# Rotary embedding: a write of zeros replaced by an early store of two rows through SyncE

## The chip, the cores and the metric

The kernel runs on one core of a Trainium2 chip. The metric is the device time of one execution in microseconds (us). Before the change the median of three runs is 319.21 us (318.87 to 319.9).

The engines that matter here are VectorE (DVE), which does the arithmetic; ScalarE (ACT), which casts; GpSimd (POOL), which only issues transfers; and SyncE (SP), which also only issues transfers. Sixteen DMA engines move all the data, whichever engine issued the transfer. Only transfers issued by POOL change the number type on the way here: loads turn float32 into float16, stores turn float16 into float32.

## The reference

The input x has the shape (8, 2048, 16, 64): batch, position, head, element. Each head's 64 elements are two halves of 32, which are rotated by an angle of the position:

```python
x1 = x[..., :32]
x2 = x[..., 32:]
out1 = x1 * cos - x2 * sin
out2 = x1 * sin + x2 * cos
out = concatenate([out1, out2], axis=-1)
```

cos and sin have the shape (2048, 32) and serve all batches and heads. The input is 64 MB of float32, and so is the output. The arithmetic in the kernel is in float16.

## The kernel before

A tile is one batch. The 2048 positions are spread over 128 partitions, J = 16 consecutive positions ("rows") for each, so a partition holds 16 x 16 x 64 = 16384 elements of a batch: 64 KB in HBM as float32, 32 KB on chip as float16. Five buffers `xt` rotate through the eight batches (`NBUF = 5`).

- **Loads.** `load(b)` (line 53) is one transfer issued by POOL. The first five are issued at the start. For batch 0 it leaves out the first `JA = 2` rows of each partition. Those come as float32 through SyncE into a buffer `head` (line 36), and ScalarE casts them into the tile (line 78). SyncE then loads the sine and cosine tables (lines 45 and 46), which ScalarE casts to float16, the sine with both signs (lines 82 to 84).
- **Rotation.** `rotate` is four DVE instructions on a whole tile: second halves times minus sine (line 70) and first halves times sine (line 71) go into a scratch buffer `v`, the tile is multiplied in place by cosine (line 73), and `v` is added (line 75). There is one buffer `v`, so the tiles follow one another.
- **Stores.** `store(b)` (line 61) is one transfer issued by POOL for batches 0 to 6. Batch 7 goes out in three parts: rows 0 to 8 (line 109), rows 9 to 13 (line 111), both through POOL, and the last two rows, which ScalarE casts into `head` (line 119) and SyncE stores as float32 once the first part has landed (line 120).
- **The write of zeros.** POOL fills a small buffer `zero` (line 86). ScalarE issues a write of it, 128 elements (512 bytes) for each partition, to the start of that partition's rows of out[0] (line 87), once load 3 has landed: `add_manual_dep` adds that wait. Store 0 writes the same place later, so it waits until the zeros have landed.

The order on each engine isn't the program's order. When the TileContext closes, a planner goes through the instructions with costs of its own. When an engine's queue comes free in its reckoning, it places the earliest in program order of those that it reckons ready there. Semaphores for the data dependences are put in afterwards. So in the program load 5, which needs the buffer of batch 0 and so store 0's landing, comes right after store 0, while on POOL the order is: loads 0 to 4, stores 0 and 1, loads 5 and 6, stores 2 and 3, load 7, stores 4, 5 and 6, and the parts of batch 7. The transfers of POOL run through one queue (q0 in the profile), those of SyncE through q1, those of ScalarE through q10. An engine that waits at an instruction holds up everything behind it on the same engine.

Of the kernel before, what the change touches and what calls it, by code (L numbers as in the profile page):

```python
# [1 line left out]

# [4 lines left out]


@with_exitstack  # L10
def kernel(
    ctx: ExitStack,
    tc: tile.TileContext,
    x: bass.AP,
    cos: bass.AP,
    sin: bass.AP,
    out: bass.AP,
):
    nc = tc.nc
    f16 = mybir.dt.float16  # L20
    f32 = mybir.dt.float32

    B, S, H, D = x.shape
    Dh = D // 2
    P = nc.NUM_PARTITIONS
    J = S // P
    NBUF = 5

    const_pool = ctx.enter_context(tc.tile_pool(name="rope_const", bufs=1))
    io_pool = ctx.enter_context(tc.tile_pool(name="rope_io", bufs=NBUF))  # L30
    tmp_pool = ctx.enter_context(tc.tile_pool(name="rope_tmp", bufs=1))

    JA = 2
    head = const_pool.tile([P, JA, H, D], f32)
    x0 = x[0].rearrange("(p j) h d -> p j (h d)", j=J)
    nc.sync.dma_start(  # L36
        out=head.rearrange("p j h d -> p (j h d)"),
        in_=x0[:, 0:JA, :].rearrange("p j f -> p (j f)"),
    )
    sin_f = const_pool.tile([P, J, Dh], f32)  # L40
    cos_f = const_pool.tile([P, J, Dh], f32)
    cos_h = const_pool.tile([P, J, Dh], f16)
    sin_h = const_pool.tile([P, J, Dh], f16)
    neg_h = const_pool.tile([P, J, Dh], f16)
    nc.sync.dma_start(out=sin_f, in_=sin.rearrange("(p j) d -> p j d", j=J))  # L45
    nc.sync.dma_start(out=cos_f, in_=cos.rearrange("(p j) d -> p j d", j=J))

    loads = []

    def load(b):  # L50
        xt = io_pool.tile([P, J, H, D], f16)
        j0 = JA if b == 0 else 0
        dma = nc.gpsimd.dma_start(  # L53
            out=xt[:, j0:J, :, :].rearrange("p j h d -> p (j h d)"),
            in_=x[b].rearrange("(p j) h d -> p j (h d)", j=J)[:, j0:J, :].rearrange("p j f -> p (j f)"),
        )
        loads.append(dma)
        return xt

    def store(b, xt):  # L60
        nc.gpsimd.dma_start(  # L61
            out=out[b].rearrange("(p j) h d -> p (j h d)", j=J), in_=xt
        )

    def rotate(xt):
        v = tmp_pool.tile([P, J, H, D], f16)
        sin_b = sin_h.unsqueeze(2).to_broadcast([P, J, H, Dh])
        neg_b = neg_h.unsqueeze(2).to_broadcast([P, J, H, Dh])
        cos_b = cos_h.unsqueeze(2).to_broadcast([P, J, 2 * H, Dh])
        nc.vector.tensor_mul(out=v[:, :, :, 0:Dh], in0=xt[:, :, :, Dh:D], in1=neg_b)  # L70
        nc.vector.tensor_mul(out=v[:, :, :, Dh:D], in0=xt[:, :, :, 0:Dh], in1=sin_b)  # L71
        xw = xt.rearrange("p j h (e d) -> p j (h e) d", d=Dh)
        nc.vector.tensor_mul(out=xw, in0=xw, in1=cos_b)  # L73
        xa = xt.rearrange("p j h d -> p (j h d)")
        nc.vector.tensor_add(out=xa, in0=xa, in1=v.rearrange("p j h d -> p (j h d)"))  # L75

    tiles = [load(b) for b in range(NBUF)]
    nc.scalar.copy(  # L78
        out=tiles[0][:, 0:JA, :, :].rearrange("p j h d -> p (j h d)"),
        in_=head.rearrange("p j h d -> p (j h d)"),  # L80
    )
    nc.scalar.copy(out=sin_h, in_=sin_f)  # L82
    nc.scalar.mul(out=neg_h, in_=sin_f, mul=-1.0)  # L83
    nc.scalar.copy(out=cos_h, in_=cos_f)  # L84
    zero = const_pool.tile([P, 128], f32)
    nc.gpsimd.memset(zero, 0.0)  # L86
    blank = nc.scalar.dma_start(
        out=out[0].rearrange("(p j) h d -> p (j h d)", j=J)[:, 0:128], in_=zero
    )
    tc.add_manual_dep(  # L90
        blank.ins,
        loads[3].ins.name,
        mybir.DependencyInfo(mybir.DependencyClass.Sync, mybir.DependencyReason.DATA),
        reason="a first write behind this load",
    )
    def part(b, j0, j1):
        return (
            out[b].rearrange("(p j) h d -> p j (h d)", j=J)[:, j0:j1, :].rearrange("p j f -> p (j f)"),
            tiles[b][:, j0:j1, :, :].rearrange("p j h d -> p (j h d)"),
        )  # L100

    for b in range(B):
        rotate(tiles[b])
        if b < B - 1:
            store(b, tiles[b])
        if b + NBUF < B:
            tiles.append(load(b + NBUF))
    dst, src = part(B - 1, 0, 9)
    gate = nc.gpsimd.dma_start(out=dst, in_=src)  # L109
    dst, src = part(B - 1, 9, J - JA)  # L110
    rest = nc.gpsimd.dma_start(out=dst, in_=src)  # L111
    tc.add_manual_dep(
        rest.ins,
        gate.ins.name,
        mybir.DependencyInfo(mybir.DependencyClass.NoSync, mybir.DependencyReason.DATA),
        reason="order of the ring",
    )
    dst, src = part(B - 1, J - JA, J)
    nc.scalar.copy(out=head.rearrange("p j h d -> p (j h d)"), in_=src)  # L119
    end = nc.sync.dma_start(out=dst, in_=head.rearrange("p j h d -> p (j h d)"))  # L120
    tc.add_manual_dep(
        end.ins,
        gate.ins.name,
        mybir.DependencyInfo(mybir.DependencyClass.Sync, mybir.DependencyReason.DATA),
        reason="the last rows go out behind this part",
    )


# [1 line left out]
_INS = ['x', 'cos', 'sin']  # L130
_OUTS = [((8, 2048, 16, 64), 'float32')]


# [23 lines left out]
```

## Time and profile before

| | before |
|---|---|
| median of three runs | 319.21 us |
| profiled execution | 319.21 us, with a span of 317.4 us |
| DVE busy | 209.2 us, 66% of the span |
| ScalarE busy | 6.8 us, 2% |
| POOL busy | 9.6 us, 3% |
| read from and written to HBM | 67.63 and 67.17 MB, 425 GB/s over the span |

An engine's busy time counts its instructions while they execute. The page of the profile cuts the span into 40 equal slices of 7.9 us and gives a digit for each: tenths of the slice in which an engine, or the mean of the 16 DMA engines, was busy. The row of waits says which engine stood still before which line, what ended the wait, how long in total, how many times, and the longest. The chain is the sequence of work that ended last, followed back from the end: start, length, what. A DMA in it lasts from its issue to its landing, so it holds the time in which it stood in a queue. In the order of time, a row gives start and length in us, the engine, the line, the operation, what is written and read, the number of instructions, and in brackets the idle time before it with what ended it. For a POOL transfer the length is that of its issue alone. The GB/s of a load are counted at its float16 side, those of a store at its float32 side.

### The profile page before, as it was taken

The numbers are of one execution on the slowest core, as the hardware profiler recorded it, in microseconds if no ns is written. First come the engines' busy times: TensorE is split into PE (matmuls) and PEld (weight loads), VectorE is DVE, ScalarE is ACT, GpSimd is POOL, SyncE is SP. The second block draws the span as 40 slices with busy tenths as digits, with TensorE's granted clock in tenths as the row PEclk, the third lists the DMA queues.
The fourth block names the chain that finished last, engine by engine and source line by source line (L and its number), as shares of the span: only waits on it lengthen the run. The fifth ranks groups of instructions, "written<-read, shape, count | busy, mean of one in ns | idle before, by whom it ended". The sixth has DMA issues, their size and how long they took to land.

```text
span 317.4 us, 131 instructions
## 1 busy us (share of the span) xinstructions
DVE 209.2 (66%) x32; ACT 6.8 (2%) x6; POOL 9.6 (3%) x22
## 2 busy tenths in 40 slices
DVE  0009599999999999999959999990008994000000
ACT  4010000000000000000000000000000002000000
POOL 4000000000000000001000000100000001000000
DMA  9899999999996999999999999999999999999998
GB/s 273 186 260 205 198 260 202 198 223 239 199 201 136 528 396 396 454 405 198 198 264 198 264 454 471 396 396 396 198 198 471 454 396 396 529 396 396 429 421 339
DMA packets 3168, 101.78 MB, mean 321 GB/s; under 512 B 352, under 2 KB 480, under 8 KB 736
## 3 DMA queue, kind: packets, MB, share of 16 engines
q0 software_dynamic: 2448, 99.09, 97.2%
q1 hardware_dynamic: 576, 2.62, 2.2%
q10 hardware_dynamic: 144, 0.07, 0.1%
HBM read 67.63 MB, written 67.17 MB: 425 GB/s over the span
## 4 chain that ended last, share of the span: by engine, by line
DMA 36%; issue 25%; another core or an unknown queue 14%; DVE 7%; ACT 1%; POOL 1%; SPq 0%; POOLq 0%; ACTq 0%; DVEq 0%
DMA xt<-in_x_dram 12%; DMA cos_f<-in_cos_dram 11%; DMA out_dram<-xt 7%; DMA out_dram<-zero 6%; DVE xt L75 3%; DVE xt L73 3%; DVE v L71 1%; ACT head L119 1%; POOL xt L53 0%; POOL out_dram L61 0%; ACT cos_h L84 0%; SPq L45 0%; SPq L36 0%; DVE v L70 0%
## 5 line engine op out<-in xcount | busy, mean ns | idle before, releaser
L73 DVE TENSOR_TENSOR xt<-xt,cos_h 128x16384 f16<-128x16384 f16 x8 | 69.5, 8692 | 3.7 <-ACT cos_h L84 3.4
L70 DVE TENSOR_TENSOR v<-xt,neg_h 128x8192 f16<-128x8192 f16 x8 | 35.4, 4425 | 52.4 <-DMA xt<-in_x_dram 52.2
L75 DVE TENSOR_TENSOR xt<-xt,v 128x16384 f16<-128x16384 f16 x8 | 69.5, 8692 | 0.3
L71 DVE TENSOR_TENSOR v<-xt,sin_h 128x8192 f16<-128x8192 f16 x8 | 35.3, 4418 | 0.0
L53 POOL DMA_DIRECT2D xt<-in_x_dram x8 | 4.4, 559 | 96.1 <-DMA out_dram<-xt 95.3
L61 POOL DMA_DIRECT2D out_dram<-xt x7 | 3.7, 535 | 110.4 <-DMA out_dram<-zero 98.1
L119 ACT CAST head<-xt 128x2048 f32<-128x2048 f16 x1 | 1.9, 1897 | 229.4 <-DVE xt L75 229.4
L109 POOL DMA_DIRECT2D out_dram<-xt x1 | 0.5, 531 | 50.5 <-DVE xt L75 50.5
L78 ACT CAST xt<-head 128x2048 f16<-128x2048 f32 x1 | 1.9, 1897 | 3.5 <-DMA head<-in_x_dram 3.5
L78 ACT ACT_TABLE_LOAD x1 | 1.3, 1283 | 0.7 <-PEq L141 0.7
L84 ACT CAST cos_h<-cos_f 128x512 f16<-128x512 f32 x1 | 0.6, 617 | 18.0 <-DMA cos_f<-in_cos_dram 18.0
L82 ACT CAST sin_h<-sin_f 128x512 f16<-128x512 f32 x1 | 0.6, 618 | 9.0 <-DMA sin_f<-in_sin_dram 9.0
L83 ACT ACTIVATE neg_h<-sin_f 128x512 f16<-128x512 f32 x1 | 0.6, 624 | 0.0
L111 POOL DMA_DIRECT2D out_dram<-xt x1 | 0.5, 531 | 0.0
L86 POOL MEMSET zero<- 128x128 f32 x1 | 0.3, 261 | 0.0
L141 POOL MEMSET const-float32-0.0<- 128x1 f32 x1 | 0.1, 99 | 0.2 <-issue 0.2
L141 POOL MEMSET const-float32-1.0<- 128x1 f32 x1 | 0.1, 99 | 0.0
L141 POOL MEMSET const-bfloat16-1.0<- 128x1 bf16 x1 | 0.1, 99 | 0.0
L141 POOL MEMSET const-uint8-127<- 128x1 uint8 x1 | 0.1, 99 | 0.0
## 6 DMA issues: line engine op xcount, KB each, us to landing
xt<-in_x_dram POOLq DMA_DIRECT2D x7, 4096.0 KB, 41.3
out_dram<-xt POOLq DMA_DIRECT2D x1, 4608.0 KB, 42.4
xt<-in_x_dram POOLq DMA_DIRECT2D x1, 3584.0 KB, 22.6
out_dram<-xt POOLq DMA_DIRECT2D x1, 2560.0 KB, 47.9
head<-in_x_dram SPq DMA_DIRECT2D x1, 1024.0 KB, 4.7
out_dram<-head SPq DMA_DIRECT2D x1, 1024.0 KB, 8.4
sin_f<-in_sin_dram SPq DMA_DIRECT2D x1, 256.0 KB, 15.2
cos_f<-in_cos_dram SPq DMA_DIRECT2D x1, 256.0 KB, 33.9
```

Source lines behind the costliest of these rows:

```text
L53: dma = nc.gpsimd.dma_start(out=xt[:, j0:J, :, :].rearrange("p j h d -> p (j h d)"), in_=x[b].rearrange("(p j) h d -> p j (h d)", j=J)[:, ...
L61: nc.gpsimd.dma_start(out=out[b].rearrange("(p j) h d -> p (j h d)", j=J), in_=xt)
L70: nc.vector.tensor_mul(out=v[:, :, :, 0:Dh], in0=xt[:, :, :, Dh:D], in1=neg_b)
L71: nc.vector.tensor_mul(out=v[:, :, :, Dh:D], in0=xt[:, :, :, 0:Dh], in1=sin_b)
L73: nc.vector.tensor_mul(out=xw, in0=xw, in1=cos_b)
L75: nc.vector.tensor_add(out=xa, in0=xa, in1=v.rearrange("p j h d -> p (j h d)"))
L78: nc.scalar.copy(out=tiles[0][:, 0:JA, :, :].rearrange("p j h d -> p (j h d)"), in_=head.rearrange("p j h d -> p (j h d)"),)
L82: nc.scalar.copy(out=sin_h, in_=sin_f)
L83: nc.scalar.mul(out=neg_h, in_=sin_f, mul=-1.0)
L84: nc.scalar.copy(out=cos_h, in_=cos_f)
L109: gate = nc.gpsimd.dma_start(out=dst, in_=src)
L119: nc.scalar.copy(out=head.rearrange("p j h d -> p (j h d)"), in_=src)
```

## The change

The zeros, their buffer and their write go. Instead the first two rows of batch 0 are rotated by themselves (four DVE instructions on 2 of the 16 rows), ScalarE casts them back into `head` as float32, and SyncE stores them to out[0]. That store carries the wait that the zeros had: load 3 has landed. The rotation of batch 0 in the loop then covers rows 2 to 15 only, and so does store 0. For this, `rotate` takes a range of rows, and `store` leaves out the first two rows for batch 0. Everything else stays.

```diff
     def store(b, xt):
+        j0 = JA if b == 0 else 0
         nc.gpsimd.dma_start(
-            out=out[b].rearrange("(p j) h d -> p (j h d)", j=J), in_=xt
+            out=out[b].rearrange("(p j) h d -> p j (h d)", j=J)[:, j0:J, :].rearrange("p j f -> p (j f)"),
+            in_=xt[:, j0:J, :, :].rearrange("p j h d -> p (j h d)"),
         )
 
-    def rotate(xt):
+    def rotate(xt, j0, j1):
         v = tmp_pool.tile([P, J, H, D], f16)
-        sin_b = sin_h.unsqueeze(2).to_broadcast([P, J, H, Dh])
...
-        nc.vector.tensor_mul(out=v[:, :, :, 0:Dh], in0=xt[:, :, :, Dh:D], in1=neg_b)
-        nc.vector.tensor_mul(out=v[:, :, :, Dh:D], in0=xt[:, :, :, 0:Dh], in1=sin_b)
-        xw = xt.rearrange("p j h (e d) -> p j (h e) d", d=Dh)
+        n = j1 - j0
+        js = slice(j0, j1)
+        sin_b = sin_h[:, js, :].unsqueeze(2).to_broadcast([P, n, H, Dh])
+        neg_b = neg_h[:, js, :].unsqueeze(2).to_broadcast([P, n, H, Dh])
+        cos_b = cos_h[:, js, :].unsqueeze(2).to_broadcast([P, n, 2 * H, Dh])
+        nc.vector.tensor_mul(out=v[:, js, :, 0:Dh], in0=xt[:, js, :, Dh:D], in1=neg_b)
+        nc.vector.tensor_mul(out=v[:, js, :, Dh:D], in0=xt[:, js, :, 0:Dh], in1=sin_b)
+        xw = xt[:, js, :, :].rearrange("p j h (e d) -> p j (h e) d", d=Dh)
         nc.vector.tensor_mul(out=xw, in0=xw, in1=cos_b)
-        xa = xt.rearrange("p j h d -> p (j h d)")
-        nc.vector.tensor_add(out=xa, in0=xa, in1=v.rearrange("p j h d -> p (j h d)"))
+        xa = xt[:, js, :, :].rearrange("p j h d -> p (j h d)")
+        nc.vector.tensor_add(out=xa, in0=xa, in1=v[:, js, :, :].rearrange("p j h d -> p (j h d)"))
...
-    zero = const_pool.tile([P, 128], f32)
-    nc.gpsimd.memset(zero, 0.0)
-    blank = nc.scalar.dma_start(
-        out=out[0].rearrange("(p j) h d -> p (j h d)", j=J)[:, 0:128], in_=zero
+    rotate(tiles[0], 0, JA)
+    nc.scalar.copy(
+        out=head.rearrange("p j h d -> p (j h d)"),
+        in_=tiles[0][:, 0:JA, :, :].rearrange("p j h d -> p (j h d)"),
+    )
+    early = nc.sync.dma_start(
+        out=out[0].rearrange("(p j) h d -> p j (h d)", j=J)[:, 0:JA, :].rearrange("p j f -> p (j f)"),
+        in_=head.rearrange("p j h d -> p (j h d)"),
     )
     tc.add_manual_dep(
-        blank.ins,
+        early.ins,
         loads[3].ins.name,
...
     for b in range(B):
-        rotate(tiles[b])
+        rotate(tiles[b], JA if b == 0 else 0, J)
```

More of the change, by code (lines that the diff above doesn't have):

```diff
@@ L60, in store @@
     def store(b, xt):
+        j0 = JA if b == 0 else 0
         nc.gpsimd.dma_start(
-            out=out[b].rearrange("(p j) h d -> p (j h d)", j=J), in_=xt
+            out=out[b].rearrange("(p j) h d -> p j (h d)", j=J)[:, j0:J, :].rearrange("p j f -> p (j f)"),
+            in_=xt[:, j0:J, :, :].rearrange("p j h d -> p (j h d)"),
         )
-    def rotate(xt):
+    def rotate(xt, j0, j1):
         v = tmp_pool.tile([P, J, H, D], f16)
-        sin_b = sin_h.unsqueeze(2).to_broadcast([P, J, H, Dh])
-        neg_b = neg_h.unsqueeze(2).to_broadcast([P, J, H, Dh])
-        cos_b = cos_h.unsqueeze(2).to_broadcast([P, J, 2 * H, Dh])
-        nc.vector.tensor_mul(out=v[:, :, :, 0:Dh], in0=xt[:, :, :, Dh:D], in1=neg_b)
-        nc.vector.tensor_mul(out=v[:, :, :, Dh:D], in0=xt[:, :, :, 0:Dh], in1=sin_b)
-        xw = xt.rearrange("p j h (e d) -> p j (h e) d", d=Dh)
+        n = j1 - j0
[6 more added lines that the diff above has]
+        xw = xt[:, js, :, :].rearrange("p j h (e d) -> p j (h e) d", d=Dh)
         nc.vector.tensor_mul(out=xw, in0=xw, in1=cos_b)
-        xa = xt.rearrange("p j h d -> p (j h d)")
-        nc.vector.tensor_add(out=xa, in0=xa, in1=v.rearrange("p j h d -> p (j h d)"))
+        xa = xt[:, js, :, :].rearrange("p j h d -> p (j h d)")
+        nc.vector.tensor_add(out=xa, in0=xa, in1=v[:, js, :, :].rearrange("p j h d -> p (j h d)"))
     tiles = [load(b) for b in range(NBUF)]
@@ L84 @@
     nc.scalar.copy(out=cos_h, in_=cos_f)
-    zero = const_pool.tile([P, 128], f32)
-    nc.gpsimd.memset(zero, 0.0)
-    blank = nc.scalar.dma_start(
-        out=out[0].rearrange("(p j) h d -> p (j h d)", j=J)[:, 0:128], in_=zero
+    rotate(tiles[0], 0, JA)
[6 more added lines that the diff above has]
+        in_=head.rearrange("p j h d -> p (j h d)"),
     )
     tc.add_manual_dep(
-        blank.ins,
+        early.ins,
         loads[3].ins.name,
         mybir.DependencyInfo(mybir.DependencyClass.Sync, mybir.DependencyReason.DATA),
-        reason="a first write behind this load",
+        reason="the first rows go out behind this load",
     )
```

## The prediction

> **What bounds the kernel now.** I read the page first, for the busy shares and the row of the DMA engines, then the waits, the chain, POOL's order of time, and last the DMA share in chosen stretches. From the page:
>
> ```profile
> DVE 209.2 (66%) x32; ACT 6.8 (2%) x6; POOL 9.6 (3%) x22
> ...
> DMA  9899999999996999999999999999999999999998
> ...
> q0 software_dynamic: 2448, 99.09, 97.2%
> q1 hardware_dynamic: 576, 2.62, 2.2%
> q10 hardware_dynamic: 144, 0.07, 0.1%
> ```
>
> No engine is busy for more than 66% of the span; the 16 DMA engines are full in every slice but one. POOL's queue q0 alone takes 97.2% of them, so the time is the transfers' time plus the moments in which q0 has nothing to give. The digit 6 is such a moment: slice 13 of 40, 95.2 to 103.2 us. The waits and POOL's order of time around it:
>
> ```profile
> POOL out_dram L61 <- DMA out_dram<-zero: 98.1, 1, 98.1
> POOL xt L53 <- DMA out_dram<-xt: 95.3, 3, 56.3
> DVE v L70 <- DMA xt<-in_x_dram: 52.2, 3, 24.8
> ```
>
> ```profile
> 102.40 1.06 POOL L61 DMA_DIRECT2D out_dram<-xt  x2 [98.14 <-DMA out_dram<-zero]
> 123.67 0.53 POOL L53 DMA_DIRECT2D xt<-in_x_dram  x1 [20.20 <-DMA out_dram<-xt]
> 142.99 0.53 POOL L53 DMA_DIRECT2D xt<-in_x_dram  x1 [18.79 <-DMA out_dram<-xt]
> 143.51 1.06 POOL L61 DMA_DIRECT2D out_dram<-xt  x2
> ```
>
> The x2 are stores 0 and 1. Tile 0 is rotated at 53.6 us (its L75 starts at 44.89 and takes 8.69), yet store 0 goes out at 102.40, because it overwrites the zeros and waits for them. The chain shows this wait on the path that ends last:
>
> ```profile
> 81.99 19.82 DMA out_dram<-zero
> 101.81 0.02 issue
> 101.83 0.04 POOLq L61
> 101.88 0.52 issue
> 102.40 20.98 DMA out_dram<-xt
> 123.38 0.28 issue
> ```
>
> Load 4, the last in the queue, is issued near 3.5 us and lands 98.2 us later (the longest landing among the x loads), at 101.7. So when store 0 is at last issued, q0 is empty. Store 1, which is queued behind store 0, lands at 142.97, 19.59 us after store 0; a store in a filled queue therefore takes 19.59, and store 0's data began at 123.38 - 19.59 = 103.8. Between 101.7 and 103.8 the DMA engines stand still: 2.1 us at the last engine. The DMA share (column before the last) in two stretches:
>
> ```profile
> 96.00:108.00 12.00, 11.93 (x3) 0.00 (x0) 1.06 (x2) 1.00 0.75 248
> 108.00:120.00 12.00, 11.97 (x3) 0.00 (x0) 0.00 (x0) 1.00 1.02 437
> ```
>
> 0.75 of 12 us leaves 3.0 us, an upper end, since packets are cut at the edges. I take 2.4, near the landings, which are exact, with a little for engines that finish before the last.
>
> **The change part by part.** *Zeros and store 0's wait go.* Store 0 now writes rows 2 to 15 of each partition, which no other transfer touches; that such strided parts are kept apart shows in batch 7, where L111 follows L109 within 0.5 us and L120 starts at 308.22 while L111's part is in flight until 314.2. So store 0 waits only for its rotation, about 62 us (below), and stands in q0 behind load 4 with some 40 us to spare: the 2.4 us go. The zeros' packets go too: q10's 0.1% of 317.4 us, 0.3 us. The memset (0.26 us) lay on an idle POOL, and ACT's issue (0.37) on an idle ACT: nothing.
>
> *Two rows through SyncE.* 1 MB leaves store 0, an eighth of 19.59 = 2.45 us saved in q0, and is moved by q1. L120 moves the same 1 MB: it lands 8.4 us after 308.22, at 316.6, 2.4 after L111's 314.2. By q1's mean, 2.2% of the span for 2.62 MB, 1 MB would take 2.8. So this costs -0.05 to +0.35; I take +0.15. SyncE's issue (0.35 us) and its wait for load 3 (81.9) hold up nothing: the only later item on SyncE is L120, at 308. The data is ready long before (about 41 us). What the new write does to load 4 beside it is unseen at this size. The nearest row: from load 0's landing (23.9) to load 3's (81.91) three loads took 19.3 us each, load 4 with the zeros beside it 19.8, 0.3 of which are their own packets. So 0 to 0.5; I take 0, since q0 and q1 share engines that are full either way.
>
> When does the early write land? The zeros, 64 KB alone, took 19.82 us, as long as load 4 itself, so a packet of another queue waits its turn behind a long POOL packet. The write, then, will land some 20 to 27 us after its issue at 82. Only L119, at 263, needs its buffer back.
>
> *One more store.* Where the queue is filled, a second store has cost its bytes and nothing more: L111 lands 6.0 us after L109, and 5 of 16 rows at 19.59 are 6.1. I price the cut of store 0 in two at nothing beyond its bytes. A rule that speaks against the change stands in the Trainium skill, "DMA: Bandwidth & Descriptors", section "Anatomy of one DMA — SWDGE path": every DMA has a fixed cost of about 2.0 us, so that by the page the further store would take back 2.0 of the gain, an estimate of 318.7.
>
> *DVE.* 8192 elements take 4.425 us and 16384 take 8.692: 0.521 ns each and 0.157 us fixed. Four instructions more add 0.63 us. Worse is their place: DVE runs in order, and the small L73 must wait for cos_h (ready at 36.14), so the two large multiplications by sine, which ran before it (23.98 to 32.75), now come behind. After 36.17: small L73 and L75 1.22 each, large L70 and L71 3.89 each, large L73 and L75 7.63 each, with gaps of 0.03: 25.6, so tile 0 ends at 61.8 instead of 53.6. DVE is 8.2 us late in tiles 0 to 4. Who waits? Store 0 has until 101. Store 1 (88.0) is due before store 0 lands, near 121. Store 2 (114.3) stands on POOL behind load 6, which goes out near 140.5. Store 3 (140.5) is due there at 141, and load 7 stands behind it, not due before store 2 lands at 198. Tile 5, which waited 3.4 us for its load (162.01), starts at 166.8 and tile 6 ends at 219.2, when L7 and stores 4 and 5 still fill q0. Tile 7's load lands at 236.7 (239.2 less the gain), after that, so L109 goes out at 263 against a turn at 294. Price 0. If this cover were gone, 8.2 us would be the cost.
>
> *ScalarE.* One cast more, 1.9 us on an engine 2% busy: nothing.
>
> *Order on POOL.* Store 0 keeps its place ahead of store 1 and load 5: store 1's tile is ready 33 us before store 0 lands, so load 5, which needs that landing, does not come between.
>
> Sum: -2.4 - 0.3 + 0.15 = -2.55. The profiled execution took 319.21 us (span 317.4 and 1.8 around it), which is also the median of the runs: 316.7. Bounds: -3.0 - 0.3 - 0.05 gives 315.9; -2.1 - 0.2 + 0.35 + 0.5 gives 317.8.
>
> **Rivals.** *Write and reads get in each other's way.* The trace has no large write beside loads. At worst the engines lose the write's own 2.45 us again: 317.2 to 319.1. Against it: 0.2 us beyond their own packets is all that the zeros cost load 4.
>
> *Store 0 waits after all, for the early write.* If the two parts of out[0] count as overlapping, as zeros and store did, the gap of 2.4 stays: 319.21 - 0.3 + 0.15 = 319.1, no change. Against it: L111 and L120.
>
> *Slower: load 5 gets ahead of store 1 on POOL.* The planner sets POOL's order anew, and program order has load 5 first. Then q0 holds store 0 alone, POOL stands at load 5 until it lands, and each landing that loads 5, 6 and 7 wait for empties the queue: 0.3 to wake, 0.5 to issue, 1.4 until data flow (102.40 to 103.8), 2.2 three times: 316.7 + 6.6 = 323.3. It decides from the point where the planner reckons store 0 to land before tile 1 is rotated; by the trace's times that is 33 us off.
>
> **How the numbers follow.** Forecast 0.72 (315.9 to 317.8); getting in the way 0.10, half of it within 0.3% of before; store 0 waits 0.09; load 5 first 0.09. About 0.3% is what a measurement here can tell from no change (318.25 to 320.17). Faster: 0.72 + 0.05 = 0.77; same: 0.05 + 0.09 = 0.14; slower 0.09. The range runs from 315.9 into the second case, 318.9, which leaves out under 2 in 10.
>
> **What would show it.** Right: no dent in the DMA row near 100 us; no wait for zeros; store 0 issued at about 62 and landing near 121; DVE's first long wait ending at cos_h; tile 5 starting without waiting for its load; stores 0 and 1 ahead of load 5. Wrong: the dent remains, with store 0 waiting for out_dram<-head; load 4 landing much past 104; POOL alternating store and load with dents after 121, 142 and 182; or POOL waiting for DVE at store 3.

## The result and the profile after

The changed kernel takes 317.46 us (median of six runs, 317.39 to 317.95) against 319.49 for the kernel before (six runs, 318.87 to 319.9). The ratio is 0.9939 with a 95% interval of 0.9926 to 0.9952: faster by 2.0 us, 0.6%. The profiled execution took 317.4 us, with a span of 315.4, where the one before took 319.21 with 317.4.

The page of the changed kernel, the DMA row and the queues:

```profile
DMA  9899999999989989999999999999999999999998
...
q0 software_dynamic: 2448, 98.04, 97.2%
q1 hardware_dynamic: 720, 3.67, 7.7%
```

The 6 in slice 13 has become a 9. The 8s in slices 12 and 15 are no pauses: a packet counts in the slice in which it starts. By the trace's single packets, those of load 4 start 2.7 to 2.9 us apart, which is one of about 2.5 and one of the early store's (0.32), and those of store 0 start 2.11 apart and take 2.15. One row is odd. q1 moves 1 MB more than before and takes 7.7% of the DMA engines' span where it took 2.2%; this comes up again below.

The waits, and then the transfers' issues in order of time, from store 0 to load 5:

```profile
POOL xt L53 <- DMA out_dram<-xt: 109.9, 3, 55.9
POOL out_dram L62 <- DVE xt L79: 98.9, 3, 56.0
...
DVE v L74 <- DMA xt<-in_x_dram: 19.9, 1, 19.9
...
DVE xt L77 <- ACT cos_h L88: 17.6, 1, 17.6
DVE v L75 <- ACT sin_h L86: 15.3, 1, 15.3
```

```profile
60.03 0.54 POOL L62 DMA_DIRECT2D out_dram<-xt  x1 [55.99 <-DVE xt L79]
...
81.98 0.35 SPq L94 DMA_DIRECT2D out_dram<-head  x1
...
86.28 0.54 POOL L62 DMA_DIRECT2D out_dram<-xt  x1 [25.70 <-DVE xt L79]
...
122.01 0.53 POOL L53 DMA_DIRECT2D xt<-in_x_dram  x1 [35.20 <-DMA out_dram<-xt]
```

Store 0 (line 62 in the changed kernel) now waits for its rotation alone and is issued at 60.03 instead of 102.40. Store 1 follows at 86.28, still ahead of load 5. Load 5 goes out at 122.01, when store 0 has landed; before, it was 123.67. Most of the gain is there by then, and nothing later gives it back: load 7 goes out at 198.82 (200.92 before).

How the time between load 3 and the end of store 0 is made up can be read from the single packets too. A transfer of POOL is 128 packets of data, eight for each of the 16 DMA engines, and 16 tiny ones at its end, one for each engine, that tell of its landing. "End" in the table is the mean of the start times of these 16. Later in both kernels a load takes 19.33 us by this measure and a store 19.32.

| us | before | after |
|---|---|---|
| end of load 3 to end of load 4 | 19.68 | 22.14 |
| end of load 4 to end of store 0 | 21.84 | 17.20 |
| sum | 41.52 | 39.34 |

Before, 21.84 - 19.32 = 2.5 us of the second row is the empty queue (the data packets themselves are 2.6 us apart, from the end of load 4's last ones to store 0's first). After, the two rows hold one load (19.33), eight packets of the early store at 0.322 each on every engine (2.58) and 14 of 16 rows of a store (16.9): 38.8. The remaining 0.5 us is time that the prediction didn't have.

### The profile page after: what moved, and what is told of

Same layout as the page of the kernel before. It is cut to its first block, busy times and chain, and to the rows that moved or that the text cites. A ratio compares the mean times of both kernels' runs of the same rounds, so it can differ in the third digit from the quotient of the medians.

```text
span 315.4 us, 136 instructions
## 1 busy us (share of the span) xinstructions
DVE 209.7 (66%) x36; ACT 8.7 (3%) x7; POOL 9.4 (3%) x21
## 3 DMA queue, kind: packets, MB, share of 16 engines
q1 hardware_dynamic: 720, 3.67, 7.7%
## 4 chain that ended last, share of the span: by engine, by line
DVE 23%; DMA 22%; issue 20%; another core or an unknown queue 17%; POOL 1%; ACT 1%; SPq 0%; POOLq 0%; ACTq 0%; DVEq 0%
DMA xt<-in_x_dram 12%; DMA cos_f<-in_cos_dram 10%; DVE xt L79 8%; DVE xt L77 8%; DVE v L75 4%; DVE v L74 3%; ACT head L127 1%; POOL out_dram L62 1%; POOL xt L53 0%; ACT cos_h L88 0%; SPq L45 0%; SPq L36 0%; POOLq L53 0%; POOLq L62 0%
## 5 line engine op out<-in xcount | busy, mean ns | idle before, releaser
L77 DVE TENSOR_TENSOR xt<-xt,cos_h 128x16384 f16<-128x16384 f16 (+2 forms) x9 | 69.7, 7744 | 17.9 <-ACT cos_h L88 17.6
L79 DVE TENSOR_TENSOR xt<-xt,v 128x16384 f16<-128x16384 f16 (+2 forms) x9 | 69.7, 7744 | 0.3
L74 DVE TENSOR_TENSOR v<-xt,neg_h 128x8192 f16<-128x8192 f16 (+2 forms) x9 | 35.5, 3950 | 20.1 <-DMA xt<-in_x_dram 19.9
L75 DVE TENSOR_TENSOR v<-xt,sin_h 128x8192 f16<-128x8192 f16 (+2 forms) x9 | 35.5, 3944 | 15.3 <-ACT sin_h L86 15.3
L127 ACT CAST head<-xt 128x2048 f32<-128x2048 f16 x1 | 1.9, 1897 | 224.8 <-DVE xt L79 224.8
L90 ACT CAST head<-xt 128x2048 f32<-128x2048 f16 x1 | 1.9, 1899 | 2.6 <-DVE xt L79 2.6
## 6 DMA issues: line engine op xcount, KB each, us to landing
xt<-in_x_dram POOLq DMA_DIRECT2D x7, 4096.0 KB, 41.2
```

Of the source, the lines that this page charges most:

```text
L74: nc.vector.tensor_mul(out=v[:, js, :, 0:Dh], in0=xt[:, js, :, Dh:D], in1=neg_b)
L75: nc.vector.tensor_mul(out=v[:, js, :, Dh:D], in0=xt[:, js, :, 0:Dh], in1=sin_b)
L79: nc.vector.tensor_add(out=xa, in0=xa, in1=v[:, js, :, :].rearrange("p j h d -> p (j h d)"))
```

## The experiments

The theory is that the whole gain is the empty queue that goes. The first rival is that the early store through SyncE brings it; the second, that something about first writes does. The runs come from three sessions, in which the kernel before had medians of 319.49, 319.03 and 319.08 us. Times of different sessions therefore compare only to about 0.5 us, and finer differences are read from the packets.

**Without the zeros, and with nothing in their place.** The code from the buffer `zero` to the added wait is taken out of the kernel before:

```diff
-    zero = const_pool.tile([P, 128], f32)
-    nc.gpsimd.memset(zero, 0.0)
-    blank = nc.scalar.dma_start(
-        out=out[0].rearrange("(p j) h d -> p (j h d)", j=J)[:, 0:128], in_=zero
-    )
-    tc.add_manual_dep(
-        blank.ins,
...
```

> The kernel before without the write of zeros; nothing goes out early, and store 0 is whole. The theory of the gap (the gain is that store 0 no longer waits, so that queue q0 never runs dry): the 2.5 us of idle DMA engines and the zeros' 0.3 go, 319.5 - 2.8 = 316.7, 0.7 below the changed kernel. The rival that the early store through SyncE brings the gain: 319.5, no change. The rival that some early write has to go ahead of the first large store: slower than the changed kernel, by an unknown amount.

It took 317.44 us (ratio 0.9951, 0.9938 to 0.9963), the same as the changed kernel. So the early store brings nothing of its own that the time shows. But the time is 0.7 above the 316.7 that the theory gave. 2.5 + 0.3 were to go; against the kernel before in the same session 1.6 went, and from the end of load 3 to the end of store 0, by the packets, 2.0. POOL's order of time and the DMA row of its page:

```profile
78.27 0.54 POOL L61 DMA_DIRECT2D out_dram<-xt  x1 [25.44 <-DVE xt L75]
121.76 0.53 POOL L53 DMA_DIRECT2D xt<-in_x_dram  x1 [42.95 <-DMA out_dram<-xt]
```

```profile
DMA  9999999999999999999999999999999999999998
```

The queue never runs dry, yet store 0 lands only 1.9 us earlier than before. The single packets show where the rest went. The packets of load 4 take 2.43 us each, all but the eighth and last on each engine, right in front of store 0, which takes 3.29 in the mean. Load 4 takes 20.19, 0.86 more than the steady 19.33; store 0 takes 19.30. I call this the price of the turn, from loads to stores. At no later turn does it show: load 6 in front of store 2 and load 7 in front of store 4 have 2.43 to the last packet, in this kernel and in the two compared.

**The zeros sooner.** The kernel before, with one index changed:

```diff
-        loads[3].ins.name,
+        loads[2].ins.name,
```

> The kernel before, with the zeros held for load 2 instead of load 3. They still go out ahead of store 0, which still waits for them, but they land near 82 us, while load 4 fills the queue. The theory of the gap: 319.5 - 2.5 = 317.0, with no dent. The rival that the zeros' packets or the SyncE store are what matters: 319.5.

317.37 us (ratio 0.9952, 0.9939 to 0.9964). POOL:

```profile
85.05 1.07 POOL L61 DMA_DIRECT2D out_dram<-xt  x2 [80.79 <-DMA out_dram<-zero]
121.79 0.54 POOL L53 DMA_DIRECT2D xt<-in_x_dram  x1 [35.67 <-DMA out_dram<-xt]
```

Store 0 still waits for the zeros, only that the wait ends at 85 while load 4 fills the queue, and 1.7 us are gained against the kernel before in the same session, with nothing else changed. The price of the turn is paid here too: load 4's last packets take 3.14.

**The gap put back.** In the changed kernel store 0 waits for the early store:

```diff
...
-            store(b, tiles[b])
+            done = store(b, tiles[b])
+            if b == 0:
+                tc.add_manual_dep(
+                    done.ins,
+                    early.ins.name,
+                    mybir.DependencyInfo(mybir.DependencyClass.Sync, mybir.DependencyReason.DATA),
...
```

(In this run and in the one with load 5 first, `store` also hands back its transfer.)

> The changed kernel, with one wait added: store 0 goes out only when the early store of the first two rows has landed. The theory of the gap: the idle stretch comes back, 317.5 + 2.5 = 320.0, and the DMA row has its dent near 104 us again. The rival that the early store brings the gain: 317.5, as the changed kernel.

319.41 us against 319.03 for the kernel before in the same session (ratio 1.0013, 1.0004 to 1.0022). The gain is gone; the prediction's price for this rival was 319.1. The time lies 0.6 below the 320.0 expected: by the packets 2.3 us are empty, and load 4 loses less than in the changed kernel (below). The dent is back:

```profile
DMA  9899999999997898999999999999999999999998
```

```profile
104.69 1.07 POOL L62 DMA_DIRECT2D out_dram<-xt  x2 [100.64 <-DMA out_dram<-head]
123.81 0.54 POOL L53 DMA_DIRECT2D xt<-in_x_dram  x1 [18.06 <-DMA out_dram<-xt]
```

**The early store beside stores.** In the changed kernel it is held for load 6:

```diff
     tc.add_manual_dep(
         early.ins,
-        loads[3].ins.name,
+        loads[6].ins.name,
```

(The call stands after the loop here, where load 6 exists.)

> The changed kernel, with the early store held for load 6 instead of load 3, so that its packets go beside stores 2 and 3 and not beside load 4. If what the prediction missed (0.6 us lost at the two rows instead of 0.15) comes from writing beside a load: 317.2 or a little below, and load 4 takes 19.4 us again. If it is the price of moving the two rows at all: 317.5, as the changed kernel.

317.75 us (ratio 0.996, 0.9948 to 0.9973), 0.3 above the other kernels without a gap, so neither alternative. The packets say why. Load 4, with no write beside it, takes not 19.4 but 20.32: the price of the turn, 0.99, is paid in full. Store 0's 14 rows take 16.89, which is 14/16 of 19.32: cutting the store in two costs nothing. Stores 2 and 3 take 41.13 with the early store among them, 2.49 more than two stores. So moving two rows costs 2.49 to 2.58 and saves 2.42, as forecast, and the 0.5 us missing in the changed kernel are not a price of moving.

**VectorE's order.** In the changed kernel the block that rotates the first two rows, casts them and stores them is moved behind the rotation of the other rows:

```diff
-    rotate(tiles[0], 0, JA)
...
         rotate(tiles[b], JA if b == 0 else 0, J)
+        if b == 0:
+            rotate(tiles[0], 0, JA)
...
```

> The changed kernel, with the first two rows of batch 0 rotated after its other rows instead of before them, so that VectorE does its large multiplications by sine while the cosine table is still on its way, as before the change. Tile 0's other rows then are done some 8 us sooner. The prediction's step that VectorE's delay is covered: 317.5, no change. The rival that the delay costs something at the end of a wait: faster, down to 317.0.

317.46 us, no change, though store 0 is issued 8 us sooner (51.95). VectorE's delay is covered, as forecast.

**Load 5 first.** The prediction's slower rival, forced:

```diff
...
-            store(b, tiles[b])
+            done = store(b, tiles[b])
+            if 1 <= b <= 3:
+                tc.add_manual_dep(
+                    done.ins,
+                    loads[b + NBUF - 1].ins.name,
+                    mybir.DependencyInfo(mybir.DependencyClass.NoSync, mybir.DependencyReason.DATA),
...
```

> The changed kernel with POOL's order forced: load 5 ahead of store 1, load 6 ahead of store 2, load 7 ahead of store 3. Loads 5 and 6 then find the queue empty when the store that they wait for has landed (store 4 still fills it for load 7). The theory of the gap, and the price of the slower rival in the prediction (2.2 to 2.5 us for each empty queue): 317.5 + 2 x 2.35 = 322.2. If an empty queue costs nothing: 317.5.

326.95 us (ratio 1.0249, 1.0233 to 1.0264), 9.5 above the changed kernel, twice what was expected. The DMA row, and POOL around the two waits:

```profile
DMA  9899999989999979899968999999899999999997
```

```profile
121.97 0.53 POOL L53 DMA_DIRECT2D xt<-in_x_dram  x1 [58.97 <-DMA out_dram<-xt]
122.49 0.54 POOL L62 DMA_DIRECT2D out_dram<-xt  x1
165.26 0.53 POOL L53 DMA_DIRECT2D xt<-in_x_dram  x1 [42.23 <-DMA out_dram<-xt]
165.77 0.54 POOL L62 DMA_DIRECT2D out_dram<-xt  x1
```

A load and a store take 43.3 us here, from 121.97 to 165.26, instead of 38.6. The packets split the 4.7: 2.94 us with no packet at all, 0.55 because the load's first packets take 2.98 instead of 2.43, and 1.24 because its last ones, in front of the store, take 3.67. So the price of the turn is not that of the first store of the execution. It comes again at loads 5 and 6, each of which starts a queue that had run empty, and no more at load 7, in front of whose start the queue was full.

**A store among the first loads.** Without the zeros, store 0 placed between loads 3 and 4:

```diff
-    tiles = [load(b) for b in range(NBUF)]
+    tiles = [load(b) for b in range(NBUF - 1)]
...
             store(b, tiles[b])
+        if b == 0:
+            tiles.append(load(NBUF - 1))
```

> The kernel without the zeros, with store 0 placed between load 3 and load 4 in POOL's queue. In the kernel without zeros the last packets of load 4, in front of the first store, took 3.3 us instead of 2.43, and later turns from load to store show nothing like it. If that is the price of the first store of the execution, wherever it stands: the last packets of load 3 become slow, those of load 4 do not, and the time stays at 317.4. If it belongs to load 4 or to a turn after five loads: it stays with load 4 or goes, 316.6. If every early turn has it: both are slow, 318.3.

317.6 us (ratio 0.9956, 0.9943 to 0.9968), about the same again, although POOL's later order has changed with it (load 5 now goes ahead of store 1, and load 7 right behind load 6). The price moves with the store: load 3's last packets take 3.02 and load 3 takes 19.93; load 4 and the later turns are clean. It is one price, at the first turn, and not a matter of load 4 or of five loads.

**A small early write.** Without the zeros, with 128 elements of batch 0 that go out where the zeros stood, but with no overlap with store 0:

```diff
     def store(b, xt):
+        c0 = 128 if b == 0 else 0
...
+            tip = const_pool.tile([P, 128], f32)
+            nc.scalar.copy(out=tip, in_=tiles[0].rearrange("p j h d -> p (j h d)")[:, 0:128])
+            first = nc.scalar.dma_start(
+                out=out[0].rearrange("(p j) h d -> p (j h d)", j=J)[:, 0:128], in_=tip
+            )
```

> The kernel without the zeros, with 128 elements of each partition of batch 0 (512 bytes, where the zeros stood) cast by ScalarE after the rotation and written through its queue behind load 3; store 0 writes the rest and waits for nothing but the rotation. If a few small writes beside load 4 soften the first store's price, as the two rows seem to do: 0.3 for the packets, 0.86 saved, 316.9, faster than both kernels. If it takes a write of the two rows' size: 317.4 + 0.3 = 317.7.

317.43 us (ratio 0.9949, 0.9937 to 0.9962). Load 4's last packets take 3.35, so small writes don't soften the turn. The time is that of the kernel without any early write, below the 317.7 expected for this case by about what the packets' 0.3 us were to cost. No kernel in the study beats the changed one by more than can be measured: those that don't let the queue run empty end at 317.37 to 317.75.

## Why the prediction was right

Step by step, with the measured terms beside the forecast ones:

| term | forecast | measured |
|---|---|---|
| empty queue before store 0 | -2.4 (-3.0 to -2.1) | -2.5 |
| zeros' packets | -0.3 | -0.3 |
| two rows from q0 to q1 | +0.15 | +0.07 to +0.16 |
| load 4 beside the early store | 0 (0 to 0.5) | +0.5 |
| sum | -2.55 | -2.2 (table above), -2.0 (median) |

- *The empty queue* was sized well, with some luck. The 19.59 us for a store was the difference of two landings; by the packets a store takes 19.32, and store 0's data began at 103.5 and not 103.8. The 2.4 was picked between 2.1 and 3.0.
- *Zeros and store 0's wait go* held. Store 0 was issued at 60.03 (forecast: about 62), with nothing between it and its rotation, and landed at 121.5 (near 121). The two parts of out[0] count as disjoint.
- *What the new write does to load 4*: this is the term that was mis-sized. I took 0, the low end of what the zeros' effect on load 4 allowed. Load 4's packets beside the early store take up to 2.62 us instead of 2.43, 0.5 in all. The range had this end; the point did not. It is the larger part of the miss: 317.46 lies 0.8 above the sum's 316.66. Of this 0.52 is the smaller gain, and 0.28 is that the sum started from 319.21, where the six runs before have a median of 319.49. The time alone would have fitted the prediction's first rival too (317.2 to 319.1). The runs without a write beside load 4 speak against that rival: there the turn to store 0 costs not less but more (0.86, and 0.99 in the run with the early store late), all of it in the last packets. The kernel before did not pay it (its last packets of load 4 took 2.44); its empty queue stood at just this place. So closing the gap, with the zeros gone, gives back 2.5 + 0.3 - 0.86, about 2.0, and not 2.8. The rival isn't wholly wrong: with store 0 held back, so that nothing stands behind load 4 in q0, load 4's eight packets on an engine, beside the early store, still last 0.41 us more in all than eight of 2.43 (0.60 in the changed kernel, 0.11 beside the zeros). So most of the 0.5 comes beside the early write and needs no store behind the load. Whether it is part of the price of the turn, paid ahead, or a price of its own, the runs don't tell apart.
- *One more store* at nothing beyond its bytes held: 16.89 for 14 of 16 rows. The 2.0 us for each DMA that the Trainium skill's "DMA: Bandwidth & Descriptors" states in "Anatomy of one DMA — SWDGE (gpsimd) path" do not show in a filled queue. At an empty one the gap is longer than that: 2.5 us without a packet in the kernel before, 2.9 in the run with load 5 first. About 0.6 of the 2.5 lies between the landing of the zeros and the issue of store 0 (101.81 to 102.40).
- *DVE*, price 0, held, and the run with the order turned round shows it. Tile 0 ended at 59.7 and not at 61.8, as cos_h came 2 us sooner; tile 5 started at 164.76 without waiting for its load, and store 3 didn't wait for VectorE.
- *Order on POOL* held. The slower rival's price did not: 2.2 us for an empty queue that restarts with a load was 4.7.
- *When the early write lands* was wrong, with no effect: 39.3 us after its issue instead of 20 to 27 (see the last section).

## What to carry to other kernels

Where one queue feeds the DMA engines all the time, look for the slice in which it is empty and ask which wait let it run out; issuing the next transfer while the last one still runs took back 1.6 to 2.0 us here, and a wait that ends earlier (the zeros behind load 2) did as much as one that goes. Count as the gain not the whole gap but the gap less what the gap was hiding, here 0.5 to 1.0 us at the turn from loads to stores. A transfer ordered so that a queue runs empty behind it costs more than the idle time that the waits show: 4.7 us where 2.2 were read off.

## What the runs showed of the hardware

The price of the turn was not expected: in a queue that started with loads, the last packets in front of the first store take 3.0 to 3.7 us instead of 2.43, once, until the queue has run empty and started with loads again. With the early store beside load 4 they take 2.6 to 2.9. Three kinds of place show it (the start, a store among the first loads, loads 5 and 6 after an empty queue), and no turn in a queue kept full does, nor does one that restarted with a store. What causes it stays open.

The landing of a small transfer can be told late. The early store, in the changed kernel:

```profile
L94 SPq DMA_DIRECT2D out_dram<-head x1: 348/348/348, 82.0 to 82.0; - x1
...
DMA to landing us min/median/max: 39.3/39.3/39.3
```

Its last data packets start 21 to 24 us after the issue, up to among store 0's first. The tiny packets that tell of the landing then take 12.7 to 14.8 us. Put in order, their 16 ends lie 4 ns ahead of those of store 0's own tiny packets, at 120.4 to 120.9, and the landing is counted at 121.3. They bring q1 to the 7.7% above. The same happened, with the same 4 ns, to the early store beside stores 2 and 3 (41.2 us) and to the 128 elements (39.7). It did not happen in the kernel before, nor with store 0 held back, where the early store landed near 104, nor with the zeros sooner, where only loads stood beside the write and its tiny packets took 0.02 us. The Trainium skill ("DMA: Bandwidth & Descriptors", "Queues, rings and completion order") says that a completion is written only after every earlier write of that DMA engine, whatever the queue. The runs agree in that other queues' writes hold it up, and go further: by these ends it waited for a whole store, most of whose packets start after its own data. In these kernels nothing needed it before ScalarE's cast of batch 7's last rows, at 263.46 in the changed kernel; whoever hangs a wait on such a landing should count the store beside it.
